# A gated FFN on one core: the stores of the second dual's output combinations, in one go or in four steps

## The chip, the cores and the metric

The kernel runs on one core of one Trainium2 chip. The metric is the device time of one execution in microseconds (us); the time before is the median of three runs, 1461.03 us (1460.68 to 1463.73). Engines: PE is TensorE, DVE is VectorE, ACT is ScalarE, POOL is GpSimd, SP is SyncE; the last two issue most DMAs.

## What is computed

One layer of a hybrid block on x (1024 tokens x 1024 channels) in f32: a mixing sub-layer (two convolutional branches, gated and merged), then the FFN that this change is in, then a last norm. Cut to the part that matters:

```python
h2 = rms_norm(x, norm_ffn_g) * (1.0 + sc2) + sh2
a, bgate = split(einsum('bsd,df->bsf', h2, w_ffn_in), 2)      # 1024 -> 2 x 2816
x = x + g2 * einsum('bsf,fd->bsd', silu(a) * bgate, w_ffn_out)  # 2816 -> 1024
return rms_norm(x, final_norm_g)
```

## The kernel before

**Products instead of blocks.** Each of the large matrix products is cut into 2 x 2 blocks and done with seven block products instead of eight (a Strassen-Winograd scheme). The products are named by digits and run in the order `PRODUCTS = "1265734"`. Each f32 operand is split into a high and a low part (fp32r), and three matmuls, high x high, high x low, low x high (lines 423, 424, 426), make one f32 product.

**The FFN's input stage** has `N_IN` = 11 duals, d = 0 to 10. One dual makes two row blocks of 128 of the hidden layer (p = 0, 1) for both token halves of 512. A product is 24 matmuls of 128 x 128 by 512 columns, twelve for each p. `in_order` (line 1287) sets the order: "1" and "2" of duals 0 and 1 and "1" of dual 2 first, then the rest of duals 0 and 1, and then dual after dual; so after dual 1 has ended with "4", dual 2 goes on with "2", "6", "5", "7", "3", "4".

**Banks.** `product` (line 435 on) adds "1", "6", "7", "4" into an `x` bank per p, "2" into a `y` bank, "5" and "3" into a `z` bank. The pool `ps` has six PSUM banks, the pool `ps2` two. `y` is always from `ps2`; `z` is from `ps` except in duals 0 and 2, where `in_product` (line 1405) takes it from `ps2` as well. In dual 2 the two `z` banks of product "5" are therefore the two `y` banks of product "2", and each can be written when its `y` sum has been read.

**What empties the banks.** `in_evac` (line 1326): line 1331, on ACT, copies the bank after "1", "6" and "5"; line 1333, on DVE, adds the `y` bank of "2" to the copy of "1"; lines 1337 and 1342, on DVE, add the banks of "7" and "3"; lines 1338 and 1350, on ACT, apply silu. The results of a dual are four tiles, `b11`, `b12`, `b21`, `b22` (each 128 x 512).

**What stores them.** `hid_set(d)` (line 1370) is a generator. It forms the seven combinations that the output stage's seven products need and stores each with `store` (line 1357). It yields three times and so has four steps: (1) combinations "1" and "2", (2) line 1377 makes `b11 - b12` on DVE and line 1378 `t2`, then "6" and "5", (3) line 1382, on DVE, then "7" and "3", (4) line 1386, then "4". `minus` is line 468. `store` takes one of three staging buffers, splits the tile with `t_split` (line 463, a cast on ACT; line 464, a subtraction on DVE) and lets POOL issue a store of 512 KB to a scratch tensor `hid` in DRAM (line 1368). A staging buffer can be filled again when its store has landed.

**What sets the order of the work.** The code is written in the order of the products; a scheduler then orders each engine's queue by what is ready, in about that order, and each engine executes its queue in order. Weights come through `next_w`, two units ahead (`AHEAD = 2`): SP loads a block (line 218), additions on DVE (lines 254, 257, 259, 301) form what a product needs, line 234 casts it on ACT (`wh`) and line 235 subtracts on DVE (`wl`).

The loop that the change is in runs over `in_order[5:]` (line 1422). After a dual's last product "4" it makes `last_set = hid_set(d)` (line 1441). For duals 1 to 9 it runs all four steps at once, `list(last_set)`; for dual 10 it runs one step and leaves the others to the output stage; dual 0's whole set is stored after product "6" of dual 1 (line 1453).

Of the kernel before, what the change touches and what calls it, by code (L numbers as in the profile page):

```python
# [131 lines left out]
def block_kernel(ctx: ExitStack, tc: tile.TileContext, x0, xT, c, vecs, ada, w_first, w_plain, w_duals,  # L132
# [6 lines left out]
    def open_pool(name, bufs, stack=None, **kw):  # L139

        p = tc.tile_pool(name=name, bufs=bufs, reuse_waits="tile", **kw)
        return p, (stack.enter_context(p) if stack else p.__enter__())

    def close(*pools):
        for p, _ in reversed(pools):
            p.__exit__(None, None, None)
# [247 lines left out]
    def modulation(i, raw=None):  # L394

        if raw is None:
            raw = load(ada[i])
        else:
            nc.sync.dma_start(raw, ada[i])
        modulation_of(i, raw)  # L400
# [65 lines left out]
    def minus(out, a, b):  # L466

        nc.vector.scalar_tensor_tensor(out=out, in0=a, scalar=-1.0, in1=b, op0=ALU.mult, op1=ALU.subtract)
# [779 lines left out]
    def norm_2_sums(m):  # L1248

        b12, b22 = ([x1[k + i][:, halves[1]] for k in range(KH)] for i in (0, KH))  # L1250
        b21 = [x1[k + KH][:, halves[0]] for k in range(KH)]
        with tc.issue_after(t_split.ins), tc.issue_after(t_split.act):
            if m == "7":
                for k in range(KH):
                    nc.vector.tensor_tensor(b12[k], b22[k], b12[k], ALU.subtract)
            los = []
            for k in range(KH):
                if m == "4":
                    with tc.issue_after(los[k - 2]) if k > 1 else ExitStack():
                        minus(b21[k], t2[k], b21[k])  # L1260
                ts[m][k] = t_pair("t" + m)
                t_split({"5": x1[k][:, halves[0]], "7": b12[k], "3": b22[k], "4": b21[k]}[m], *ts[m][k])
                los.append(t_split.ins)
        norm_2_sums.ins = t_split.ins

    N_IN = FC // 2
# [90 lines left out]
    def store(key, src):  # L1357

        hid_dram[key] = dram.tile([P, T], F32R, name="hid" + "_".join(map(str, key)))
        if key[0] == N_IN - 1:  # L1360
            hl = t_pair("hid")
            t_split(src, *hl)
            for t, s in zip(hl, halves):
                nc.gpsimd.dma_start(hid_dram[key][:, s], t)
            return
        s = stagep.tile([P, T], F32R, tag="stage", name="stage")
        t_split(src, s[:, :H], s[:, H:])
        nc.gpsimd.dma_start(hid_dram[key], s)  # L1368

    def hid_set(d):  # L1370

        (b11, b12), (b21, b22) = ((ha[2 * d + p, "4"], ha[2 * d + p, "6"]) for p in range(2))
        store((d, "1"), b11)
        store((d, "2"), b21)
        yield
        t2 = gip.tile([P, H], F32, tag="g", name="t2")
        nc.vector.tensor_tensor(b11, b11, b12, ALU.subtract)
        minus(t2, b11, b22)
        store((d, "6"), t2)
        store((d, "5"), b11)  # L1380
        yield
        nc.vector.tensor_tensor(b12, b22, b12, ALU.subtract)
        store((d, "7"), b12)
        store((d, "3"), b22)
        yield
        minus(b21, t2, b21)
        store((d, "4"), b21)
# [12 lines left out]
    def in_product(d, m, between=None):  # L1400
        late = EARLY[d] == 1
        if late and m == "2":
            for p in range(2):
                in_evac(d)(p, "1", in_banks[d]["x", p])
        product(in_banks[d], m, ts[m], None if late and m == "1" else in_evac(d), between,
                z_tile=ps2_tile if d in (0, 2) else ps_tile)
        if d == N_IN - 1:
            group_load(0, m)
# [13 lines left out]
    for i, (d, m) in enumerate(in_order[5:]):  # L1422
        if i < 4:
            norm_2_sums("5734"[i])
        elif i == 4:
            close(*phase_1)
            rawap = open_pool("raw_a", 1, side="right", stack=ctx)[1]
            raws.append(rawap)
            x1aps = [s2p, open_pool("x1a", 1, side="right", stack=ctx)[1]]
            phase_2 = [open_pool("gi", 7), open_pool("stage", 3, side="right")]  # L1430
            gip, stagep = (p for _, p in phase_2)
        with ExitStack() as order:
            if d < 2:
                order.enter_context(tc.issue_after(mm3.ins))
            in_product(d, m)
        if m == PRODUCTS[-1]:
            if 2 <= d < 6:
                with tc.issue_after(in_evac.ins):
                    for b in range(40 + 2 * (d - 2), 42 + 2 * (d - 2)):
                        modulation(b, x1aps[b % 2].tile([P, T], F32, tag="x1", name="ada"))  # L1440
            last_set = hid_set(d)
            if 0 < d < N_IN - 1:
                list(last_set)
            elif d:
                next(last_set)
            if d == N_IN - 2:
                close(phase_2.pop())
                x1bp = open_pool("x1b", 3, side="right", stack=ctx)[1]
                x1 = {j: (x1aps[j] if j < 2 else x1bp).tile([P, T], F32, tag="x1", name=f"x1{j}") for j in (0, 1, 4, 5, 2)}
                for j in x1:  # L1450
                    nc.gpsimd.dma_start(x1[j], x1_dram[j])
        elif (d, m) == (1, "6"):
            list(hid_set(0))


    ng2 = cp.tile([P, KC], F32, name="ng2")
# [270 lines left out]
```

## Time and profile before

| | |
|---|---|
| median of three runs | 1461.03 us (1460.68, 1461.03, 1463.73) |
| the profiled execution's own time | 1460.71 us |
| its span in the profile | 1458.8 us, 17721 instructions |
| granted TensorE clock, mean | 0.999 |
| the FFN's input stage | about 818 to 1236 us |
| the FFN's output stage | about 1236 us to the end |
| transfers | 259.77 MB in all, mean 178 GB/s |

The profile is of one execution; its span is the time between the first and the last instruction, the execution's time has a little around it. A row of the timeline has the start in us, the duration in us, the engine, the line, the operation, what it writes and reads, and in square brackets how long the engine had been idle and what ended that. Starts are from the span's start. TensorE's matmuls are pipelined and their ends are modelled, so two matmuls in a row overlap in the rows; the distance of their starts is the true pace.

### The profile page before, as it was taken

Reading aid. Unit: us, or ns where it says so; the run is one execution under the profiler, and the core shown is the slowest. Engines: PE = TensorE matmul, PEld = TensorE weight load, DVE = VectorE, ACT = ScalarE, POOL = GpSimd, SP = SyncE. Lnnn points to the kernel's source line nnn. Section 1 sums busy time; section 2 is a strip of 40 time slices with the busy share of each in tenths; the row PEclk is TensorE's granted clock in tenths of the full one; section 3 lists DMA queues with packets and bytes.
Section 4 is the critical chain, followed back from the end, with each engine's and each line's share of the span. In section 5 each row is a group of like instructions: output and inputs, shape, how many; then the busy total and the mean of one; then the engine's idle time right before and its main releaser. Section 6 shows DMA issues by size and latency. Waiting matters only on the chain.

```text
span 1458.8 us, 17721 instructions
## 1 busy us (share of the span) xinstructions
PE 1446.8 (99%) x6394; PEld 1188.5 (81%) x6394; DVE 1180.6 (81%) x1628; ACT 629.3 (43%) x911; POOL 513.4 (35%) x474
## 2 busy tenths in 40 slices
PE   9999999999999999999999999999999999999997
PEld 5888888888888888888888888888888888888887
DVE  7897999987988978989688798877776665866676
ACT  4773332333333346555235465434444443322235
POOL 0007777677677762001022001101110105662505
PEclk9999999999999999999999999999999999999999
DMA  9542132323222359666595437555454449996903
GB/s 361 202 147 87 59 102 72 116 73 101 73 87 73 130 201 323 175 221 208 188 316 197 133 101 266 196 173 186 161 187 141 142 145 347 396 375 187 360 1 116
DMA packets 90122, 259.77 MB, mean 178 GB/s; under 512 B 10241, under 2 KB 12929, under 8 KB 90034
## 3 DMA queue, kind: packets, MB, share of 16 engines
q1 hardware_dynamic: 45808, 145.18, 29.9%
q0 software_dynamic: 40192, 100.87, 21.6%
q10 hardware_dynamic: 4034, 12.59, 2.3%
q8 instruction: 50, 0.82, 0.2%
q14 instruction: 38, 0.31, 0.1%
HBM read 193.06 MB, written 65.54 MB: 177 GB/s over the span
## 4 chain that ended last, share of the span: by engine, by line
PE 95%; POOL 1%; DMA 1%; issue 1%; DVE 0%; ACT 0%; POOLq 0%; ACTq 0%
PE bank L423 12%; PE bank L426 12%; PE bank L424 12%; PE x L426 8%; PE x L423 8%; PE x L424 8%; PE z L423 3%; PE z L426 3%; PE z L424 3%; PE y L426 2%; PE y L423 2%; PE y L424 2%; PE mix L424 2%; PE yb L424 2%; PE yb L426 2%; PE mix L423 2%
## 5 line engine op out<-in xcount | busy, mean ns | idle before, releaser
L234 ACT CAST wh<-raw 128x1024 fp32r<-128x1024 f32 (+3 forms) x255 | 261.2, 1026 | 483.5 <-PE bank L424 149.1
L235 DVE TENSOR_TENSOR wl<-raw,wh 128x1024 fp32r<-128x1024 f32 (+3 forms) x176 | 207.3, 1180 | 64.1 <-ACT wh L234 58.5
L235 POOL TENSOR_TENSOR wl<-raw,wh 128x1024 fp32r<-128x1024 f32 x79 | 191.9, 2431 | 106.0 <-ACT wh L234 102.9
L1004 DVE SCALAR_TENSOR_TENSOR c<-diff,vec,c 128x512 f32<-128x512 f32 x232 | 168.2, 751 | 2.7
L1368 POOL DMA_DIRECT2D hid<-stage x70 | 37.3, 533 | 345.6 <-DVE stage L464 334.9
L426 PE MATMUL bank<-th,wl 128*128 128x512 f32 x312 | 121.4, 389 | 0.0
L423 PE MATMUL bank<-th,wh 128*128 128x512 f32 x312 | 121.4, 389 | 0.0
L424 PE MATMUL bank<-tl,wh 128*128 128x512 f32 x312 | 121.4, 389 | 0.0
L1004 DVE SCALAR_TENSOR_TENSOR c<-u,wsum,c 128x512 f32<-128x512 f32 x112 | 84.2, 752 | 2.3
L424 PE MATMUL x<-tl,wh 128*128 128x512 f32 x176 | 68.5, 389 | 0.0
L423 PE MATMUL x<-th,wh 128*128 128x512 f32 x176 | 68.5, 389 | 0.0
L426 PEld LDWEIGHTS bank<-th,wl 128*128 128x128 f32 x312 | 58.6, 188 | 12.2
L423 PEld LDWEIGHTS bank<-th,wh 128*128 128x128 f32 x312 | 58.6, 188 | 12.1
L424 PEld LDWEIGHTS bank<-tl,wh 128*128 128x128 f32 x312 | 58.6, 188 | 12.1
L426 PE MATMUL x<-th,wl 128*128 128x512 f32 x176 | 68.4, 390 | 0.0
L464 DVE TENSOR_TENSOR stage<-g,stage 128x512 fp32r<-128x512 f32 x60 | 41.1, 688 | 27.8 <-ACT stage L463 27.7
L463 ACT CAST stage<-g 128x512 fp32r<-128x512 f32 x60 | 37.3, 622 | 55.4 <-DMA hid<-stage 40.8
L1392 POOL DMA_DIRECT2D th<-hid x77 | 41.2, 536 | 53.9 <-PE x L426 32.8
L312 POOL TENSOR_TENSOR raw<-raw 128x1024 f32<-128x1024 f32 x8 | 21.0, 2626 | 106.9 <-ACT th L463 102.8
L426 PE MATMUL yb<-zsh,wl 128*128 128x512 f32 x128 | 49.8, 389 | 0.0
L424 PE MATMUL yb<-zsl,wh 128*128 128x512 f32 x128 | 49.8, 389 | 0.0
L423 PE MATMUL yb<-zsh,wh 128*128 128x512 f32 x128 | 49.8, 389 | 0.0
(830 smaller groups left out, 4123.5 us busy)
## 6 DMA issues: line engine op xcount, KB each, us to landing
hid<-stage POOLq DMA_DIRECT2D x70, 512.0 KB, 4.8
raw<-in_w_duals SPq DMA_DIRECT2D x57, 512.0 KB, 3.5
raw<-in_w_fi SPq DMA_DIRECT2D x54, 512.0 KB, 4.3
th<-hid POOLq DMA_DIRECT2D x77, 256.0 KB, 6.0
tl<-hid POOLq DMA_DIRECT2D x77, 256.0 KB, 6.0
ada<-in_ada SPq DMA_DIRECT2D x24, 512.0 KB, 5.6
raw<-in_ada SPq DMA_DIRECT2D x24, 512.0 KB, 4.6
raw<-in_w_fo SPq DMA_DIRECT2D x16, 512.0 KB, 6.2
```

Of the source, the lines that this page charges most:

```text
L234: hi = nc.scalar.copy(wh, raw)
L235: lo = lo_engine.tensor_tensor(wl, raw, f32(wh), ALU.subtract)
L312: unit.eng.tensor_tensor(out, x, y, ALU.add)
L423: nc.tensor.matmul(ps, wh, xh, start=first, stop=False, skip_group_check=again)
L424: nc.tensor.matmul(ps, wh, xl, start=False, stop=False, skip_group_check=again)
L426: mm3.ins = nc.tensor.matmul(ps, wl, xh, start=False, stop=last, skip_group_check=again).ins
L463: t_split.act = nc.scalar.copy(hi, src).ins
L464: t_split.ins = nc.vector.tensor_tensor(lo, src, f32(hi), ALU.subtract).ins
L1004: tap.ins = nc.vector.scalar_tensor_tensor(out=out, in0=src[:, s : s + H], scalar=wt, in1=acc, op0=ALU.mult, op1=ALU.add).ins
L1368: nc.gpsimd.dma_start(hid_dram[key], s)
L1392: nc.gpsimd.dma_start(t, hid_dram[key][:, s])
```

## The change

Dual 1's set is no longer run in one go. After product "4" of dual 1 only step 1 is run, and after each of the next products of dual 2 ("2", "6", "5") one more step; after "7" and "3" the generator is exhausted, and `next(last_set, None)` does nothing. At dual 2's own "4" the old branch applies again. Dual 0 and duals 2 to 10 are as before.

```diff
@@ -1439,7 +1439,7 @@
                     for b in range(40 + 2 * (d - 2), 42 + 2 * (d - 2)):
                         modulation(b, x1aps[b % 2].tile([P, T], F32, tag="x1", name="ada"))
             last_set = hid_set(d)
-            if 0 < d < N_IN - 1:
+            if 1 < d < N_IN - 1:
                 list(last_set)
             elif d:
                 next(last_set)
@@ -1451,6 +1451,8 @@
                     nc.gpsimd.dma_start(x1[j], x1_dram[j])
         elif (d, m) == (1, "6"):
             list(hid_set(0))
+        elif d == 2:
+            next(last_set, None)


     ng2 = cp.tile([P, KC], F32, name="ng2")
```

The lists of PE and SP stay as they were, and POOL issues the same DMAs in the same order. On DVE and ACT the work between product "2" and product "7" of dual 2 is ordered anew. On DVE, before (`g_7269` is `b11` of dual 1, `g_7085` and `g_7099` its `b12` and `b22`, `g_7284` its `b21`, `t_7297` its `t2`; `y` are the banks of dual 2's product "2"; `wl` are weights of dual 2's "7" and "3"):

```order
L1377 TENSOR_TENSOR g_7269<-g_7269,g_7085 128x512
L1333 TENSOR_TENSOR g_7327<-y,g_7327 128x512
L468 SCALAR_TENSOR_TENSOR t_7297<-g_7269,g_7099 128x512
L1382 TENSOR_TENSOR g_7085<-g_7099,g_7085 128x512
L468 SCALAR_TENSOR_TENSOR g_7284<-t_7297,g_7284 128x512
L464 TENSOR_TENSOR stage<-t_7297,stage 128x512
L464 TENSOR_TENSOR stage<-g_7269,stage 128x512
L464 TENSOR_TENSOR stage<-g_7085,stage 128x512
L1333 TENSOR_TENSOR g_7329<-y,g_7329 128x512
L235 TENSOR_TENSOR wl<-raw,wh 128x1024 x2
```

And now, in the same place (`t_7333` is `t2`; the copies of "1" are `g_7297` and `g_7299`):

```order
L1333 TENSOR_TENSOR g_7297<-y,g_7297 128x512
L1377 TENSOR_TENSOR g_7269<-g_7269,g_7085 128x512
L1333 TENSOR_TENSOR g_7299<-y,g_7299 128x512
L468 SCALAR_TENSOR_TENSOR t_7333<-g_7269,g_7099 128x512
L235 TENSOR_TENSOR wl<-raw,wh 128x1024
L464 TENSOR_TENSOR stage<-t_7333,stage 128x512
L464 TENSOR_TENSOR stage<-g_7269,stage 128x512
L1382 TENSOR_TENSOR g_7085<-g_7099,g_7085 128x512
L468 SCALAR_TENSOR_TENSOR g_7284<-t_7333,g_7284 128x512
L464 TENSOR_TENSOR stage<-g_7085,stage 128x512
L235 TENSOR_TENSOR wl<-raw,wh 128x1024
```

The second addition of L1333 has moved from behind three staging subtractions (L464) to a place ahead of all of them, the weights of "7" ahead of `t2`'s staging, and L1382 with the L468 behind it to after two stagings. On ACT, before (`x` and `z` are banks of dual 2, the copies are those of "6", "6" and "5"; `wh` are weights of dual 2):

```order
L463 CAST stage<-t_7297 128x512
L463 CAST stage<-g_7269 128x512
L463 CAST stage<-g_7085 128x512
L1331 COPY g_7379<-x 128x512
L234 CAST wh<-raw 128x1024
L463 CAST stage<-g_7099 128x512
L1331 COPY g_7393<-x 128x512
L463 CAST stage<-g_7284 128x512
L1331 COPY g_7413<-z 128x512
L234 CAST wh<-raw 128x1024
L1331 COPY g_7428<-z 128x512
```

And now:

```order
L463 CAST stage<-t_7333 128x512
L463 CAST stage<-g_7269 128x512
L1331 COPY g_7362<-x 128x512
L463 CAST stage<-g_7085 128x512
L234 CAST wh<-raw 128x1024
L1331 COPY g_7376<-x 128x512
L463 CAST stage<-g_7099 128x512
L1331 COPY g_7407<-z 128x512
L463 CAST stage<-g_7284 128x512
L234 CAST wh<-raw 128x1024
L1331 COPY g_7422<-z 128x512
```

Each of the first three copies has moved ahead of one cast; the second copy of `z`, the last row, still stands behind all of them and behind a weight cast.

## The prediction

> **What bounds the kernel now.** I read the page's shares first, then the chain that ended last, then who the tensor engine waited for, then the rows around the one wait that is left. From the page, the busy row and the chain's share by engine:
>
> ```profile
> PE 1446.8 (99%) x6394; PEld 1188.5 (81%) x6394; DVE 1180.6 (81%) x1628; ACT 629.3 (43%) x911; POOL 513.4 (35%) x474
> PE 95%; POOL 1%; DMA 1%; issue 1%; DVE 0%; ACT 0%; POOLq 0%; ACTq 0%
> ```
>
> TensorE is busy for 1446.8 of 1458.8 us and is 95% of the chain. The whole room left is 12 us, and a change that removes no matmul can only give back a part of that. Which part, the list of TensorE's waits says (engine, tile, line, what released it: us in total, times, longest):
>
> ```profile
> PE clock L616 <- DVE ones_r L634: 1.6, 1, 1.6
> PE z L423 <- DVE g L1333: 1.2, 1, 1.2
> PE clock L616 <- DVE newton L678: 0.7, 1, 0.7
> ```
>
> The two on `clock` belong to the start of the program. So in the FFN stages there is exactly one wait: a matmul into a `z` bank that is held up by line 1333, VectorE's addition that empties a `y` bank. TensorE's own rows there (start, duration, engine, line):
>
> ```profile
> 910.81 0.39 PE L426 MATMUL z<-t5h,wl 128*128 128x512 f32 x1
> 912.44 0.50 PE L423 MATMUL z<-t5h,wh 128*128 128x512 f32 x1 [1.24 <-DVE g L1333]
> 912.78 0.40 PE L424 MATMUL z<-t5l,wh 128*128 128x512 f32 x1
> 913.01 0.39 PE L426 MATMUL z<-t5h,wl 128*128 128x512 f32 x1
> ...
> 915.29 0.39 PE L423 MATMUL x<-t7h,wh 128*128 128x512 f32 x1
> ```
>
> This is product "5" of the third dual (d = 2): its second `z` half should have begun one pitch after 910.81. The pitch comes from the product before it, whose first row is at 902.88 and whose successor begins at 908.32, 24 matmuls later: 5.44 / 24 = 0.2267 us.
>
> ```profile
> 900.16 0.39 PE L423 MATMUL y<-h24h,wh 128*128 128x512 f32 x1
> ...
> 902.65 0.39 PE L426 MATMUL y<-h27h,wl 128*128 128x512 f32 x1
> 902.88 0.39 PE L423 MATMUL x<-t2h,wh 128*128 128x512 f32 x1
> ...
> 908.32 0.39 PE L423 MATMUL z<-t5h,wh 128*128 128x512 f32 x1
> ```
>
> From 910.81 to 915.29 there are 13 pitches, 2.95 us, and 4.48 us went by. **The wait costs 1.53 us**: 1.40 until the matmul starts, the rest in the rows just behind it. The label's 1.24 is shorter because the modelled ends overlap the next start; I use the starts.
>
> Why was the bank not free? Its matmuls were all issued by 902.65. The chain of waits shows what it hung on:
>
> ```profile
> 904.44 5.89 DMA hid<-stage
> ...
> 910.43 0.63 ACT stage L463
> ...
> 911.09 0.04 DVE stage L464
> 911.13 0.57 issue
> 911.70 0.70 DVE g L1333
> 912.39 0.04 issue
> 912.44 0.50 PE z L423
> ```
>
> A store of the second dual must land before its staging buffer can take the next combination; ScalarE's cast (L463) waits for that, VectorE's subtraction (L464) waits for the cast, and the bank's addition (L1333), which needs none of this, stands behind that subtraction in VectorE's queue. The queue itself:
>
> ```profile
> 903.16 0.69 DVE L464 TENSOR_TENSOR stage<-g,stage 128x512 fp32r<-128x512 f32 x1
> 903.76 0.69 DVE L1377 TENSOR_TENSOR g<-g,g 128x512 f32<-128x512 f32 x1
> 904.37 0.69 DVE L1333 TENSOR_TENSOR g<-y,g 128x512 f32<-128x512 f32 x1
> 904.97 0.68 DVE L468 SCALAR_TENSOR_TENSOR t<-g,g 128x512 f32<-128x512 f32 x1
> 905.57 0.69 DVE L1382 TENSOR_TENSOR g<-g,g 128x512 f32<-128x512 f32 x1
> 906.17 0.69 DVE L468 SCALAR_TENSOR_TENSOR g<-t,g 128x512 f32<-128x512 f32 x1
> 906.77 0.69 DVE L464 TENSOR_TENSOR stage<-t,stage 128x512 fp32r<-128x512 f32 x1
> 909.11 0.69 DVE L464 TENSOR_TENSOR stage<-g,stage 128x512 fp32r<-128x512 f32 x1 [1.65 <-ACT stage L463]
> 911.09 0.69 DVE L464 TENSOR_TENSOR stage<-g,stage 128x512 fp32r<-128x512 f32 x1 [1.28 <-ACT stage L463]
> 911.70 0.68 DVE L1333 TENSOR_TENSOR g<-y,g 128x512 f32<-128x512 f32 x1
> 912.30 2.35 DVE L235 TENSOR_TENSOR wl<-raw,wh 128x1024 fp32r<-128x1024 f32 x2
> ```
>
> The first `y` half is read at 904.37; the second, ready at about the same time, only at 911.70, behind three staging subtractions.
>
> **The change, part by part.** It removes and adds no instruction; TensorE's list is the same row for row. What moves stands between 903 and 917 us on VectorE and ScalarE.
>
> VectorE, evacuations. Both additions of L1333 now come first: one ahead of L1377, the other right behind it. VectorE's slot for a 512-wide operation is 0.60 us (903.76 to 904.37). So they start at 903.76 and 904.97, and the second bank is free at 904.97 + 0.68 = 905.65. The second `z` half wants it at 908.32 + 12 x 0.2267 = 911.04: 5.4 us in hand. The first is free at 904.45 for a use at 908.32. **The wait goes whole: -1.53 us.**
>
> VectorE, the rest. The subtraction that makes `t2` (L468) has one more addition ahead of it, so it starts at 905.57 instead of 904.97; behind it now comes the split of product "7"'s weights (L235), then `t2`'s staging subtraction. The row of 912.30 gives 2.35 us for two splits, so one holds the queue some 1.18 us: 906.17 to 907.35. The `t2` staging starts at 907.35 instead of 906.77, 0.58 later. The next two staging subtractions wait for stores issued earlier, so 909.11 and 911.09 stand. L1382 and the second L468, moved behind 909.11, take 909.71 to 910.9, in time for a cast that waited until 910.43 anyway. Nothing on TensorE waits for any of these: cost nothing. The split for "7" is ready at 907.4 instead of 913.5; "7" now starts at 915.29 - 1.53 = 913.76. Here the change gives room just where the earlier start needs it.
>
> ScalarE and the stores. These rows are ScalarE's, and behind the dots GpSimd's store issues:
>
> ```profile
> 902.85 1.06 ACT L234 CAST wh<-raw 128x1024 fp32r<-128x1024 f32 x1 [0.69 <-PE y L424]
> 905.73 0.62 ACT L463 CAST stage<-t 128x512 fp32r<-128x512 f32 x1 [1.82 <-DVE t L468]
> 908.46 0.62 ACT L463 CAST stage<-g 128x512 fp32r<-128x512 f32 x1 [2.11 <-DMA hid<-stage]
> 911.44 1.05 ACT L234 CAST wh<-raw 128x1024 fp32r<-128x1024 f32 x1
> 916.22 0.58 ACT L1331 COPY g<-z 128x512 f32<-128x512 f32 x1
> ...
> 907.75 0.53 POOL L1368 DMA_DIRECT2D hid<-stage  x1 [2.78 <-DVE stage L464]
> 910.10 0.53 POOL L1368 DMA_DIRECT2D hid<-stage  x1 [1.81 <-DVE stage L464]
> ```
>
> The `x` copies of product "6" move ahead of the third and fourth casts, and the first `z` copy of "5" ahead of the fifth. GpSimd issues the same seven stores in the same order; only the third, `t2`'s, moves, by the 0.58 us worked out above, from 907.75 to 908.33. SyncE's weight loads keep their order. The added risk is that the `z` copies still stand behind casts that wait for stores, while TensorE comes 1.53 us earlier. How long a store takes, from its line's answer (min, median, max of the 70):
>
> ```profile
> DMA to landing us min/median/max: 2.9/4.8/7.5
> ```
>
> First `z` copy: behind the fourth cast, which waits for the store issued at 908.33. Landing is 911.2 to 915.8, then 0.62 and 0.58: done by 917.0 at worst. Product "3" wants that bank at 913.76 + 5.44 = 919.20. Second `z` copy: behind the fifth cast (store issued at 910.10, landing by 917.6 at worst), a weight cast of 1.05 and its own 0.58, with overlaps about 2.05 us together: done by 919.7 at worst, wanted at 919.20 + 2.72 = 921.92. At the median landing, 914.9, it is done by 917.0, as it is now (916.22 + 0.58 = 916.80). The bounds for this term are 0 and, by the slowest landing seen, still 0; I take 0.
>
> Is the gain kept to the end? The waits view for the time after 880 us puts the weight casts behind TensorE itself:
>
> ```profile
> ACT wh L234 <- PE x L424: 83.2, 38, 4.8
> ```
>
> The preparation of weights runs as far ahead as its buffers allow and is let on by TensorE's own progress; it moves forward with it. No later wait of TensorE exists that could swallow 1.5 us. I keep all of it; the bounds are 0 and 1.53.
>
> Sum: 0 - 1.53 + 0 + 0. The profiled execution took 1460.71 us (span 1458.8), so it would take 1459.18. The three timed runs have a median of 1461.03, 0.32 above it; on that scale **1459.5 us, -0.10%**. That is half of what a measurement of this kernel can tell from no change, about 0.2%, or 2.9 us.
>
> [...]
>
> **The rivals.** (1) *The banks, not the queue.* Were the pair of banks itself too few, the wait would stay and the time be 1461.0. Against it: the second `y` bank had its last matmul issued at 902.65 and was read at 911.70; from 904.97 on, VectorE was at staging work, or waiting for it, all the time, and the change puts that work behind the addition. This is also what a change without effect would look like, and the order shows the rows moved. 4%.
>
> (2) *The gap moves.* TensorE comes earlier and is stopped at the next thing that is not paced by itself, so that half or all is given back: 1460.3 to 1461.0. For it: ScalarE's casts still wait for stores. Against it: the margins above, 2.2 us at the slowest landing seen. 10%.
>
> (3) *Slower: a late store holds the second `z` bank.* The place is ScalarE's fifth cast, with a weight cast and the bank's copy queued behind it. It decides from the point where the store issued at 910.10 lands later than 921.92 - 2.05 = 919.87, 9.8 us after issue; every us beyond is a us of TensorE. To be more than 0.2% slower it must also eat the gain: 1.53 + 2.92 = 4.45 us more, a landing after 14.2 us, giving 1464.0 or more. The slowest of 70 took 7.5. 4%.
>
> **How the numbers follow.** Forecast (the wait gone, nothing new): 82%. Rivals 1 to 3: 4, 10 and 4%. The three runs of before span 1460.68 to 1463.73. The range takes the highest less 1.53, 1462.2, and below the median three times the 0.35 us by which the lowest run lies under it, 1461.03 - 1.05 - 1.53 = 1458.4; it holds rivals 1 and 2. Faster by over 0.2% needs 1458.1 or less, 1.4 us more than the wait can give: only a scatter of the reading does that, 10%. Slower by over 0.2% is rival 3 with its 4%, and 2% for a high reading of the forecast's time. The rest, 84%, is within 0.2%.
>
> **What would show it.** Right: no row `PE z <- DVE g L1333` among TensorE's waits; both L1333 of the third dual before 906 us; "7" starting at 913.8; busy time of TensorE unchanged and the span 1.5 us shorter. The step on ScalarE is right if the copies of "5" end before 919.2 and 921.9. Wrong: a wait on `z` for ScalarE's L1331 near 919 or 922 us (rivals 2, 3), or the same wait at 912 with L1333 read early (rival 1).

## The result, and the profile after

The changed kernel takes 1459.66 us (median of 11 runs, 1458.58 to 1461.64). The kernel before, run beside it, has a median of 1464.13 us (11 runs, 1460.68 to 1465.93). The ratio is 0.9975, with a 95% interval of 0.9965 to 0.9984: faster by a quarter of a per cent, or some 4 us (the medians lie 4.47 us apart). The predicted time (1459.5) and its range hold; the predicted gain, 1.53 us, was too small. The profiled execution took 1458.58 us, its span is 1456.6. Two executions far off the rest, one of run 1 (1611.84 us) and one of the kernel before beside runs 5 to 8 (5196.95 us), are left out of the ratios below.

The page of the changed kernel, in the two lines that answer to those of before, shows a TensorE that does the same 6394 matmuls in a span shorter by 2.2 us. Its busy time, forecast as unchanged, is 1.3 us lower; what makes that up is not shown.

```profile
PE 1445.5 (99%) x6394; PEld 1187.4 (82%) x6394; DVE 1182.0 (81%) x1628; ACT 628.4 (43%) x911; POOL 514.4 (35%) x474
PE 97%; POOL 1%; DVE 0%; issue 0%; POOLq 0%
```

TensorE's waits in the changed kernel are all on `clock`, at the program's start; the wait on `z` is gone:

```profile
PE clock L616 <- DVE ones_r L634: 1.6, 1, 1.6
PE clock L616 <- DVE newton L678: 0.7, 1, 0.7
PE clock L616 <- ACT sq L575: 0.4, 1, 0.4
```

VectorE's rows at the place (start, duration, engine, line) have both additions of L1333 ahead of the stagings:

```profile
904.20 0.69 DVE L1333 TENSOR_TENSOR g<-y,g 128x512 f32<-128x512 f32 x1
904.80 0.69 DVE L1377 TENSOR_TENSOR g<-g,g 128x512 f32<-128x512 f32 x1
905.40 0.69 DVE L1333 TENSOR_TENSOR g<-y,g 128x512 f32<-128x512 f32 x1
906.00 0.69 DVE L468 SCALAR_TENSOR_TENSOR t<-g,g 128x512 f32<-128x512 f32 x1
906.60 1.23 DVE L235 TENSOR_TENSOR wl<-raw,wh 128x1024 fp32r<-128x1024 f32 x1
907.74 0.69 DVE L464 TENSOR_TENSOR stage<-t,stage 128x512 fp32r<-128x512 f32 x1
```

And TensorE passes from the first `z` half to the second, and on to "7", without a step in its starts:

```profile
910.20 0.39 PE L426 MATMUL z<-t5h,wl 128*128 128x512 f32 x1
910.43 0.39 PE L423 MATMUL z<-t5h,wh 128*128 128x512 f32 x1
...
913.15 0.39 PE L423 MATMUL x<-t7h,wh 128*128 128x512 f32 x1
```

From 910.20 to 913.15 are 2.95 us, the 13 pitches that took 4.48 before. Of the 2.2 us between the two spans, 1.53 are here; nearly all of the rest, 0.61, lies ahead of the change: TensorE's first matmul of the FFN stage behind the sum of the norm starts at 818.33 us in the trace before and at 817.72 in this one.

So one question is left: at the place of the change the profiles differ by the 1.53 us that were predicted, and the medians differ by three times as much.

### The profile page after: what moved, and what is told of

Same layout as the page of the kernel before. It is cut to its first block, busy times and chain, and to the rows that moved or that the text cites. A ratio compares the mean times of both kernels' runs of the same rounds, so it can differ in the third digit from the quotient of the medians.

```text
span 1456.6 us, 17721 instructions
## 1 busy us (share of the span) xinstructions
PE 1445.5 (99%) x6394; PEld 1187.4 (82%) x6394; DVE 1182.0 (81%) x1628; ACT 628.4 (43%) x911; POOL 514.4 (35%) x474
## 4 chain that ended last, share of the span: by engine, by line
PE 97%; POOL 1%; DVE 0%; issue 0%; POOLq 0%
PE bank L424 12%; PE bank L423 12%; PE bank L426 12%; PE x L426 8%; PE x L423 8%; PE x L424 8%; PE z L426 4%; PE z L423 4%; PE z L424 4%; PE y L426 2%; PE y L424 2%; PE y L423 2%; PE mix L426 2%; PE yb L426 2%; PE yb L423 2%; PE mix L424 2%
## 5 line engine op out<-in xcount | busy, mean ns | idle before, releaser
L235 DVE TENSOR_TENSOR wl<-raw,wh 128x1024 fp32r<-128x1024 f32 (+3 forms) x176 | 207.8, 1182 | 56.3 <-ACT wh L234 50.6
L235 POOL TENSOR_TENSOR wl<-raw,wh 128x1024 fp32r<-128x1024 f32 x79 | 191.9, 2432 | 105.9 <-ACT wh L234 105.9
L423 PE MATMUL bank<-th,wh 128*128 128x512 f32 x312 | 121.4, 389 | 0.0
L423 PEld LDWEIGHTS bank<-th,wh 128*128 128x128 f32 x312 | 58.6, 188 | 12.2
L423 PE MATMUL x<-th,wh 128*128 128x512 f32 x176 | 68.5, 389 | 0.0
L464 DVE TENSOR_TENSOR stage<-g,stage 128x512 fp32r<-128x512 f32 x60 | 41.3, 690 | 28.5 <-ACT stage L463 28.3
L423 PE MATMUL yb<-zsh,wh 128*128 128x512 f32 x128 | 49.8, 389 | 0.0
```

The lines of the kernel that those rows point to most:

```text
L235: lo = lo_engine.tensor_tensor(wl, raw, f32(wh), ALU.subtract)
L423: nc.tensor.matmul(ps, wh, xh, start=first, stop=False, skip_group_check=again)
L464: t_split.ins = nc.vector.tensor_tensor(lo, src, f32(hi), ALU.subtract).ins
```

## The experiments

**Theory Q** (queue): the wait on `z` is as long as the read of the second `y` bank is late in VectorE's queue. **Theory E**: the rest of the gain lies elsewhere. After the first four runs, two of which show a granted clock of 0.57 behind a wait, a **theory C** (clock) joined: a long enough wait also costs speed behind it. Ratios are to the kernel before, run on the same chip (medians 1462.81, 1463.12 and 1464.23 us in the three batches).

### 1. The kernel before, once more

No edit.

> The kernel before, unchanged, for its scatter. Theory Q (queue): what varies between its executions (1460.7 to 1465.9 us) is the one wait on z of the third dual, since it hangs on when stores land; the time less that wait is steady at 1459.2 +- 1. So a profile that lasts 1464 us shows that wait at about 5 us, one of 1461 us at about 1.5 us. Theory E (elsewhere): the wait is always near 1.5 us, and the other 3 us lie in another place (the start, the end, a wait of another stage). Time against the kernel before: 1.000.

Measured: 1463.33 us (1460.90 to 1466.49), ratio 1.0006 (0.9997 to 1.0015). The profiled execution took 1465.34 us, span 1463.4. The two longest of TensorE's waits in it, both longer than in the first trace:

```profile
PE clock L616 <- ACT sq L575: 2.2, 1, 2.2
PE z L423 <- DVE g L1333: 2.2, 1, 2.2
```

TensorE's rows behind the wait on `z` show something that the first trace did not have:

```profile
912.90 0.39 PE L426 MATMUL z<-t5h,wl 128*128 128x512 f32 x1
915.47 0.50 PE L423 MATMUL z<-t5h,wh 128*128 128x512 f32 x1 [2.18 <-DVE g L1333]
915.81 0.57 PE L424 MATMUL z<-t5l,wh 128*128 128x512 f32 x1
916.17 0.63 PE L426 MATMUL z<-t5h,wl 128*128 128x512 f32 x1
916.60 0.63 PE L423 MATMUL z<-t5h,wh 128*128 128x512 f32 x1
...
918.73 0.63 PE L426 MATMUL z<-t5h,wl 128*128 128x512 f32 x1
919.16 0.45 PE L423 MATMUL z<-t5h,wh 128*128 128x512 f32 x1
919.45 0.39 PE L424 MATMUL z<-t5l,wh 128*128 128x512 f32 x1
...
919.91 0.40 PE L423 MATMUL x<-t7h,wh 128*128 128x512 f32 x1
```

From 915.81 to 919.16 the starts lie up to 0.43 us apart instead of 0.23. The table by stretches (stretch, its length, busy time of PE, PEld, DVE, ACT and POOL, granted clock, DMA share, GB/s) shows the granted clock fall in the same stretch. TensorE counts as busy for 3.93 of its 4.00 us, so busy time does not show this loss:

```profile
910.00:915.40 5.40, 3.29 (x15) 2.40 (x13) 2.46 (x5) 2.55 (x4) 1.35 (x3) 1.00 0.83 300
915.40:919.40 4.00, 3.93 (x10) 3.15 (x11) 3.49 (x5) 2.14 (x5) 0.78 (x2) 0.57 0.85 272
919.40:924.00 4.60, 4.60 (x21) 3.77 (x21) 3.01 (x4) 1.53 (x2) 0.53 (x1) 1.00 0.88 328
```

From 912.90 to 919.91 go 7.01 us, where 13 pitches are 2.95: this execution lost 4.06 us at the place, 2.34 until the matmul starts and 1.72 behind it. Against the changed kernel's trace that is most of the 6.8 us between the spans; the same matmul of the FFN stage as above also starts 2.71 us later, at 820.43. Theory Q expected a wait of about 5 us in so long an execution, and 2.34 us is too little; theory E is wrong for the greater part: more than half of the difference is at the place, but it is not the wait alone.

### 2. Other banks for the late `z`

```diff
         product(in_banks[d], m, ts[m], None if late and m == "1" else in_evac(d), between,
-                z_tile=ps2_tile if d in (0, 2) else ps_tile)
+                z_tile=ps2_tile if d == 0 else ps_tile)
```

> The kernel before with one edit: product 5 of the third dual takes its z banks from the pool of six, so they are no longer the y banks; the orders of VectorE, ScalarE, GpSimd and SyncE are the same row for row, and the second y bank is still read late. Theory Q: no wait of TensorE there, time as that of the changed kernel, 1459 to 1460 us, ratio 0.9975 +- 0.001. Theory E: at most 1.5 us less than before, ratio 0.999. Rival (the new order of VectorE and ScalarE itself saves something): ratio clearly nearer 1 than the changed kernel's.

Measured: 1459.64 us (1458.68 to 1460.52), ratio 0.9976 (0.9967 to 0.9985). The second `y` bank is read as late as ever:

```profile
911.73 0.68 DVE L1333 TENSOR_TENSOR g<-y,g 128x512 f32<-128x512 f32 x1
```

but TensorE does not wait for it any more (its second `z` half starts at 910.42 us, 0.23 behind the matmul before), and the whole gain of the change is there without any of its new order. So, within these intervals (some 1.3 us to either side), all that the change brings comes from this one wait and what follows it; a saving by VectorE's and ScalarE's new order itself does not show.

### 3. The read behind all seven stagings

```diff
+                with tc.issue_after(t_split.ins) if (d, p) == (2, 1) else ExitStack():
-                nc.vector.tensor_tensor(ha[f, "1"], ps, ha[f, "1"], ALU.add)
+                    nc.vector.tensor_tensor(ha[f, "1"], ps, ha[f, "1"], ALU.add)
```

> The kernel before with the addition that reads the second y bank ordered behind all seven stagings of the second dual instead of behind five. Theory Q: the wait on z grows to about 5.0 us in an execution like the profiled one (read at about 915.2 instead of 911.7 us), 3.5 us more; time 1464 to 1469 us, ratio 1.001 to 1.003. Theory E: the wait is hidden again further on or the median does not follow it: ratio within 0.001 of 1.

Measured: 1464.08 us (1462.21 to 1465.68), ratio 1.0009 (1.0000 to 1.0018). Slower by less than the wait was meant to grow, and hardly clear of no difference: the scheduler answered by putting eight matmuls of "7" ahead of the second `z` half, and the stop moved to those, which wait for a copy on ScalarE behind the casts:

```profile
PE x L423 <- ACT g L1331: 2.6, 1, 2.6
PE x L426 <- DVE wl L235: 0.5, 1, 0.5
PE z L423 <- DVE g L1334: 0.2, 1, 0.2
```

By the starts, TensorE stood still for 2.76 us before those matmuls. The granted clock behind that was 0.57 again (913.5 to 917.5 us), as in run 1 (the line numbers here are one higher below the edit), and matmul starts lay 0.43 us apart there. It is no clean dose of the wait, but it shows the same fall of the clock.

### 4. In one go, one product later

```diff
-            if 0 < d < N_IN - 1:
+            if 1 < d < N_IN - 1:
                 list(last_set)
-            elif d:
+            elif d == N_IN - 1:
                 next(last_set)
...
         elif (d, m) == (1, "6"):
             list(hid_set(0))
+        elif (d, m) == (2, "2"):
+            list(last_set)
```

> The second dual's set is stored in one go, but begun one product later, after product 2 of the third dual instead of after product 4 of the second; no four steps. Theory Q: both reads of y come ahead of the stagings, no wait, ratio 0.9975 +- 0.001 as for the changed kernel. Rival (the spread over four products is what counts, fewer casts in front of the copies on ScalarE): a wait on z or x near 914 to 922 us, ratio nearer to 1.

Measured: 1458.68 us (1458.58 to 1460.46), ratio 0.9972 (0.9963 to 0.9981), and no wait of TensorE in the FFN (the second `z` half starts at 912.28 us, 0.23 behind the matmul before). The four steps are not needed: it is enough that the second read of `y` (at 907.96 us here) comes ahead of `t2`'s staging and of those behind it, which wait for stores.

### 5. The read behind four stagings

This is an edit of the changed kernel. The first two steps run before product "2", the others behind it, and the read is ordered behind the fourth staging (`t_split.ins` is kept as `fourth` there):

```diff
+            if d == 1:
+                next(last_set)
+                fourth = t_split.ins
...
+                    if (d, p) == (2, 1):
+                        order.enter_context(tc.issue_after(fourth))
```

> The second dual's first four stagings stand before product 2 of the third dual, the last three behind it in steps, and the read of the second y bank is ordered right behind the fourth staging: behind one store's landing less than before the change. Theory Q (the wait is how late that read is): read at about 909.7 to 910.4 us on the scale of the profile before, wanted at 911.0, so a wait of 0 to 0.3 us and a time within 0.5 us of the changed kernel, 1459 to 1460 us. Theory C (a wait of TensorE costs more than its length, since the granted clock falls for some 3.4 us behind it: 0.43 us a matmul instead of 0.23): the same, as so short a wait leaves the clock alone. Theory E (what is gained comes from the new order elsewhere): a time between before and after.

Measured: 1460.06 us (1458.59 to 1463.01), ratio 0.9982 (0.9973 to 0.9991). The trace has the read at 909.10 us (expected: 909.7 to 910.4) and no wait. So the read may stand behind four stagings and still come in time; behind the fifth, as before the change, it does not. That the ratio lies a little nearer to 1 than the others fits reads that come too late in some executions, but no trace of such a one was taken.

### 6 and 7. A longer wait

Scalings of a tile that nobody reads (128x248) on VectorE, between the fifth staging and the read: three in run 6, where a split of weights (L235) slips in among them, and one in run 7.

```diff
+                    if (d, p) == (2, 1):
+                        last = fifth[0]
+                        for _ in range(IDLE_OPS):
+                            with tc.issue_after(last):
+                                last = nc.vector.tensor_scalar(fill_t, fill_t, 1.0, None, ALU.mult).ins
+                        order.enter_context(tc.issue_after(last))
```

> The kernel before with three small scalings of an unused tile (128x248) on VectorE between the fifth staging and the read of the second y bank; a weight split slips in between them, so the read is some 2.0 to 2.3 us later than before. Theory Q alone: the wait is 3.5 to 4.5 us and costs just that: some 4 us more than the changed kernel, 1463 to 1464 us, ratio to before 1.0000 to 1.0010. Theory C: the clock falls to half behind the wait in every execution and costs 1.6 us on top: 1464.8 to 1466 us, ratio 1.0013 to 1.0022; the profile shows matmul starts 0.43 us apart for some 3.4 us behind the wait and a granted clock below 0.7 in that stretch.

> The same with one scaling instead of three, and no weight split in front: the read is 0.3 us later than before. Theory Q alone: 0.3 us more than before, ratio 1.0002. Theory C: in some executions the wait is now long enough to pull the clock down, so up to 1.6 us more on top in those: median 0.3 to 1.5 us above before, and executions between two levels some 1.6 us apart.

Measured, three scalings: 1465.26 us (1464.44 to 1466.76), ratio 1.0016 (1.0007 to 1.0024); the lowest of these runs is above theory Q's 1464. Its wait (with line numbers raised by the edit, L425 for L423 and L1342 for L1333), and the stretch behind it:

```profile
PE z L425 <- DVE g L1342: 4.6, 1, 4.6
...
909.00:914.80 5.80, 1.74 (x8) 1.12 (x6) 3.28 (x7) 3.90 (x7) 1.48 (x3) 1.00 0.74 266
914.80:918.40 3.60, 3.02 (x8) 2.34 (x9) 2.86 (x4) 0.79 (x2) 0.68 (x2) 0.62 0.90 264
```

One scaling: 1463.32 us (1460.61 to 1464.99), ratio 1.0007 (0.9997 to 1.0016). Here the wait was 2.72 us by the starts, and the clock did not fall:

```profile
PE z L425 <- DVE g L1342: 2.6, 1, 2.6
...
913.90:917.50 3.60, 3.55 (x16) 2.94 (x17) 3.47 (x4) 2.65 (x5) 0.47 (x2) 1.00 0.78 241
```

Run 6 settles theory C against Q alone: TensorE lost 6.53 us there, 4.80 until the matmul starts and 1.73 behind it, with a clock of 0.62. Where the clock held at 1.00, only some 0.1 us was lost behind the wait (0.13 in the first trace and in run 7), so the clock costs 1.6 us in run 6, as in run 1. Run 7 shows that a wait of 2.72 us need not do that, while 2.34 us did in run 1.

### 8. Two staging buffers, before the change

```diff
-            phase_2 = [open_pool("gi", 7), open_pool("stage", 3, side="right")]
+            phase_2 = [open_pool("gi", 7), open_pool("stage", 2, side="right")]
```

> The kernel before with two staging buffers instead of three: casts wait for an earlier store each. Theory Q: the stagings in front of the read of the second y bank are now four, not five, but each waits longer; the read comes at 909 to 913 us, a wait of 0 to 2 us; further waits of TensorE near 903 us where weights stand behind stagings are possible, 0 to 2 us. Time 1459 to 1465 us. Theory C: behind each wait of 2 us or more a stretch with matmuls 0.43 us apart.

Measured: 1461.51 us (1460.16 to 1463.38), ratio 0.9993 (0.9984 to 1.0002). With fewer buffers the scheduler put the read behind the third staging (expected: the fourth) instead of the fifth, and the wait on `z` is gone. In its place are two on copies of later duals, 0.93 us at 954.9 and 0.43 us at 993.6:

```profile
PE x L423 <- ACT g L1331: 1.1, 2, 0.8
```

Losing a buffer cost the kernel before nothing that can be measured: new waits of 1.36 us stand against a wait that is gone. No execution of this run has a mean granted clock below 0.998.

### 9 to 12. The changed kernel, the late set and the kernel before again, and rival 3 provoked

Runs 9 and 12 are the changed kernel and the kernel before as they are, run 10 is run 4's kernel, run 11 the changed kernel with the edit of run 8.

> The changed kernel, unchanged, on the same chip as the next run. Theory Q with C: no wait of TensorE in the FFN stages, 1458.6 to 1461.6 us; what scatter is left lies ahead of 818 us, in the waits at the program's start.

> The second dual's set in one go, one product later, for comparison with the changed kernel on one chip. Theory Q: neither has a wait of TensorE in the FFN, so both are the same within 0.5 us, and the 1 us between their medians so far comes from the start. Rival: storing in one go is better by 1 us.

> The changed kernel with two staging buffers instead of three, which makes every cast wait for a store that was issued later: the prediction's rival 3, provoked. Theory Q: no wait on z at 912 us, but the waits of TensorE near 955 and 994 us on copies (L1331) that stand behind casts, as in the kernel before with two buffers, 1.5 us together; 1460 to 1462 us. Rival 3: the wait also shows on z or x of the third dual between 913 and 925 us, 1 us or more.

> The kernel before, for a third trace of it. Theory C: the wait on z is 1.4 to 3 us by how late the fifth store lands; behind a wait of more than 2 us matmul starts may be 0.43 us apart for up to 3.4 us. Theory Q alone: never slower matmuls behind the wait.

Measured: run 9, 1458.92 us (1458.62 to 1460.16), ratio 0.9969 (0.9957 to 0.9981); run 10, 1459.33 us (1458.52 to 1460.46), ratio 0.9969 (0.9958 to 0.9980), so the two ways to order the set are the same within the scatter. Run 11: 1459.65 us (1459.18 to 1460.17), ratio 0.9971 (0.9960 to 0.9982). Its only wait of TensorE in the FFN, 0.5 us by the starts, is at 992.6:

```profile
PE x L423 <- ACT g L1331: 0.3, 1, 0.3
```

Between 913 and 925 us there is none: with two staging buffers, too, no copy of a `z` or `x` bank of the third dual came too late.

Run 12 took 1461.13 us, span 1459.2. Its wait is 2.40 us by the starts, and the clock stayed at 1.00 behind it (the store that decides is the second of the set, for which the fifth staging waits):

```profile
PE z L423 <- DVE g L1333: 2.2, 1, 2.2
...
912.40:916.00 3.60, 3.19 (x14) 2.62 (x15) 3.60 (x5) 2.80 (x6) 0.61 (x2) 1.00 0.67 209
```

Nearly the same wait as in run 1, without the fall of the clock: 2.57 us lost here, 4.06 there.

How often the clock falls can be read from the mean granted clock that each execution has on record, to three digits. The traces with a slow stretch (runs 1, 3 and 6) have 0.996 or 0.997, all others 0.998 or 0.999; a stretch like that of run 1, 3.35 us with starts 0.43 instead of 0.23 us apart, should lower the mean by about 0.0011 (3.35 x 0.47 / 1460, an estimate). Of 70 executions of kernels without the wait on `z` (the changed kernel, runs 2, 4, 5, 8, 9, 10 and 11) none is below 0.998. Of 88 executions of the kernel before (run 1 and the three batches), 46 are, with a median of 1463.95 us; the other 42 have 1462.24 us. In run 3 it is 6 of 10, in run 6 it is 10 of 11, in run 7 it is 5 of 10, with medians of 1463.94 and 1462.55 us for run 7's two groups. So about half of the executions of the kernel before lose the 1.6 us of the clock on top of the wait; the rounding makes the count a rough one.

## Why the prediction was right, and where not

**The bound, and the place: right.** TensorE bounds the kernel (busy for 99% of the span before), and one wait was left to remove. Run 2 removes that wait alone and gets the same time.

**The cause: right.** The read of the second bank stood behind stagings that wait for stores. The second store's landing took 5.89 us in all three traces of the kernel before. The rows of the chain of waits, for runs 1 and 12:

```profile
907.48 5.89 DMA hid<-stage
...
904.82 5.89 DMA hid<-stage
```

It was issued 3.88, 2.93 and 2.87 us before product "5" began (904.44 and 908.32 in the first trace), and the waits are 1.40, 2.34 and 2.40 us. Each pair adds up to 5.27 or 5.28: from the store's issue to the second `z` half it is always 8.00 or 7.99 us (the landing and three operations), and the first half covers twelve pitches, 2.72 us, of that. The later the store is issued, the longer the wait.

**The steps on VectorE, ScalarE and the stores: right.** The reads start at 904.20 and 905.40 (forecast 903.76 and 904.97), `t2`'s staging at 907.74 (907.35), "7" at 913.15 (913.76, in a trace that is 0.61 us earlier at 818 us). ScalarE's rows in the changed kernel:

```profile
914.60 0.62 ACT L463 CAST stage<-g 128x512 fp32r<-128x512 f32 x1 [1.40 <-DMA hid<-stage]
915.12 0.58 ACT L1331 COPY g<-z 128x512 f32<-128x512 f32 x1
915.93 0.62 ACT L463 CAST stage<-g 128x512 fp32r<-128x512 f32 x1 [0.22 <-DMA hid<-stage]
916.46 1.05 ACT L234 CAST wh<-raw 128x1024 fp32r<-128x1024 f32 x1
917.41 0.58 ACT L1331 COPY g<-z 128x512 f32<-128x512 f32 x1
```

The two copies of `z` end at 915.7 and 918.0 us; "3" starts at 918.59 and wants the second bank at 921.3. The margins, 2.9 and 3.3 us, lie between the 2.2 us forecast for the slowest landing and the 4.9 that its median landing gives. Casts do wait for stores here, as rival 3 said, but nothing comes late, and run 11 could not make it late either. Rival 1 (the banks are too few) is half right: more banks also cure it, as run 2 shows, but so does the order, with the same two banks.

**The size: the term that failed is "The wait goes whole: -1.53 us".** It was sized from one execution and taken for the kernel. In the three traces of the kernel before, the loss at the place is 1.53, 4.06 and 2.57 us, and the profiled execution, at 1460.71 us, was near the lowest of its kernel's runs. Two things were not in the sum.

The first is that the length of the wait varies, since VectorE's chain of stagings hangs on stores and does not keep a fixed distance from TensorE. Counted from that matmul of the FFN stage (818.33, 820.43 and 817.71 us), VectorE's L1377 of the first dual starts at 61.40, 61.39 and 61.39 us in the three traces, that of the second dual at 85.43, 86.37 and 86.44. In between stand the stagings of the first dual's set, whose casts wait for earlier stores (the cast of the sixth for 2.25 us in the first trace). The sixth of them, in the three traces, is already late by as much (73.69, 74.63 and 74.69 us, counted the same way):

```profile
892.02 0.69 DVE L464 TENSOR_TENSOR stage<-g,stage 128x512 fp32r<-128x512 f32 x1 [1.30 <-ACT stage L463]
895.06 0.69 DVE L464 TENSOR_TENSOR stage<-g,stage 128x512 fp32r<-128x512 f32 x1 [1.22 <-ACT stage L463]
892.40 0.69 DVE L464 TENSOR_TENSOR stage<-g,stage 128x512 fp32r<-128x512 f32 x1 [1.47 <-ACT stage L463]
```

The second is that TensorE's granted clock can be low behind the wait: in runs 1 and 6 for 3.35 us each (915.81 to 919.16 and 915.78 to 919.13), at up to 0.2 us a matmul, which cost 1.6 us; and by the recorded clocks (46 of 88 below 0.998) in about half of the executions of the kernel before. The prediction took the 12 us in which TensorE is not busy for the whole room; this loss lies inside its busy time. With the size, the sentence that faster by over 0.2% is only a scatter of the reading fell too, and the 10% rested on it; with the interval of 0.9965 to 0.9984, whether the gain is over 0.2% is itself not settled.

**That the time came out so well is in part luck.** The 1.53 us were taken from 1461.03, the median of three runs. The median of eleven is 1464.13, and the same sum from there gives 1462.60, above the stated range. The base was 3.10 us too low and the gain 2.94 us too small, and the two nearly cancel. They are related: the profiled execution and the median of the three runs were both from the low end, and a low execution less its own loss still lands where the changed kernel does.

**What stays open.** From that matmul of the FFN stage on, the traces differ in nothing else: the span, less that matmul's start, less the loss at the place, is 638.94, 638.91 and 638.92 us in the three traces of the kernel before and 638.88 in the changed kernel's. What varies besides the place is the program's start, common to all these kernels (2.71 us in run 1). The medians lie 4.5 and 5.3 us apart in the two comparisons of the changed kernel itself, and the largest loss traced in the kernel before is 4.06 us; whether longer waits or late starts make up the rest is not shown. Nor is it shown what decides whether the clock falls behind a given wait.

## What to carry to other kernels

A wait of the engine that bounds the kernel should be sized from several executions, and above all where it ends on a transfer: the profile's one execution may be the kindest (its wait was 1.40 us here, those of the next two traces 2.34 and 2.40). A read that frees a bank belongs ahead of work that waits for buffers, in the queue that it shares with it (here VectorE's); moving the read, giving the late user other banks or shifting the whole set by one product all gave the same here (ratios of 0.9975, 0.9976 and 0.9972). And a gap in TensorE's rows can be worth more than its length: with a granted clock of 0.57 behind it, the gap of 2.34 us in run 1 cost 4.06. The busy share did not tell this (3.93 of 4.00 us); the mean granted clock of an execution, 0.996 or 0.997 against 0.998 or 0.999, did, and it is on record even where there is no trace.

## What was not expected of the hardware

A wait of 2.34 us (run 1) was followed by 3.35 us in which matmul starts lay up to 0.43 us apart instead of 0.23 (915.81 to 919.16 us; granted clock 0.57 in the stretch of 4.00 us around it). One of 4.80 us (run 6) was followed by a slow stretch of the same length (915.78 to 919.13 us; 0.62 from 914.8 to 918.4 us), and one of 2.76 us (run 3) by starts 0.43 us apart as well (0.57 from 913.5 to 917.5 us). Waits of 1.40, 2.40 and 2.72 us (the first trace, runs 12 and 7) were followed by none: the granted clock was 1.00 behind them. So the length of the wait alone does not decide.
